# A Winograd-style convolution on one core: the last input pair through the SyncE queue, and paired stores

## The chip, the cores and the metric

The kernel runs on one NeuronCore of a Trainium2 chip. The core has TensorE (PE in the profile) for matmuls, VectorE (DVE), ScalarE (ACT), GpSimd (POOL) and SyncE (SP). Data moves between HBM and SBUF, the memory of 128 partitions on the core, through 16 DMA engines, which take their work from queues; here SyncE issues most transfers, and GpSimd can issue some, which may change the data type on the way. The metric is the device time of one execution in microseconds (us). Five runs before the change gave 127.62 to 128.03 us, with a median of 127.85.

## What is computed

A 3x3 convolution with padding 1 over 16 images of 64 channels and 64x64 pixels, to 128 channels, in fp32:

```python
def setup_inputs():
    batch, c_in, h, w, c_out = 16, 64, 64, 64, 128
    return {
        "x": np.random.randn(batch, c_in, h, w).astype(np.float32),
        "weight": np.random.randn(c_out, c_in, 3, 3).astype(np.float32) * 0.1,
    }

def reference(x, weight):
    x_pad = np.pad(x, ((0, 0), (0, 0), (1, 1), (1, 1)), mode='constant')
    ...
    output[b, co] += weight[co, ci, kh, kw] * x_pad[b, ci, kh:kh+h, kw:kw+w]
    ...
```

## The kernel before

The images are taken in 8 pairs. A pair fills the 128 partitions: 64 channels of the first image, then 64 of the second. A partition's row of one image is 64x64 fp32 values, 16 KB, so a pair of inputs is 2.1 MB; a pair of outputs is twice that, since there are 128 output channels, each in a partition of its own.

Two output rows are computed together from four input rows. The middle row of the kernel is applied once to the sum of two neighbouring rows (`ss`, made by `sums`, L93), and the result `ut` is added to two partial results, one for the even and one for the odd output row. The weights are combined to five sets `G0, G21, G1, G01, G2` in `Wt` (L103 to L124). Inputs of the matmuls are fp16, sums are fp32 in PSUM.

The loop at L135 runs over the pairs `p`, the loop at L146 over four blocks of 16 output rows. In a block, `group` (L149) issues the matmuls of L176 for both images: first `U` from `ss[p]`, then `A` and `Bt` from `xs[p]`, the pair in fp16. ScalarE copies `U` to `ut` (L190), VectorE adds `A + ut` (L196) and `Bt + ut` (L199) into the output tile `ots[p][b2]`, one tile for each image. Between these, ScalarE casts pieces of later pairs from fp32 to fp16 (`cast`, L66, in the order that `casts` lists at L129 to L133; two pieces go to GpSimd, L64), so that pair `p + 1` or `p + 2` is being cast while pair `p` is computed. GpSimd makes the sums of pair `p + 1` at the start of pair `p` (L140).

Transfers: SyncE loads the weights (L51), pair 0 in four cuts of rows, and pairs 1 to 6 in one transfer each (`load`, L55), all in fp32, ahead of everything else on its queue. Pair 7 comes another way: in pair 0, GpSimd issues one transfer that casts to fp16 on the way (`load_cast`, L78, called at L145) into the tile `xc`, so that no engine has to cast it, and GpSimd's sums for pair 7 read `xc`. When the fourth block of a pair is done, SyncE stores each image by a transfer of its own (L204); the last pair is stored in two halves of rows, so there are 14 stores of 2 MB and 4 of 1 MB. SyncE issues its transfers in the order written; a store waits for VectorE's last add.

Space: `big` has nine slots of 16 KB in each partition, handed out in turn by `next_slot` (L46). Pairs 0 to 6 take slots 0 to 6; the outputs take two slots a pair, beginning with 7 and 8 and then using again those of inputs that have been cast and of outputs that have been stored. `keep` holds the order of instructions on an engine as they are written.

Of the kernel before, what the change touches and what calls it, by code (L numbers as in the profile page):

```python
# [8 lines left out]
F32 = mybir.dt.float32  # L9
F16 = mybir.dt.float16  # L10
# [3 lines left out]
def kernel(  # L14
# [6 lines left out]
    nc = tc.nc  # L21
    B, CI, H, W = x.shape
    CO = weight.shape[0]
    assert H == 64 and W == 64 and CI == 64 and CO == 128 and B % 2 == 0
    NP = B // 2
    RB = 8

    keep = tc.keep_in_program_order
    x_rows = x.rearrange("b c h w -> (b c) h w")
    out_rows = out.rearrange("b co h w -> b co h w")  # L30
    w_flat = weight.rearrange("co ci kh kw -> co (ci kh kw)")

    const = ctx.enter_context(tc.tile_pool(name="const", bufs=1))
# [1 line left out]
    xpool = ctx.enter_context(tc.tile_pool(name="xpool", bufs=1))  # L35
    big = ctx.enter_context(tc.tile_pool(name="big", bufs=1))
# [2 lines left out]

    NH = 7
    slot = [0]

    def next_slot(shape, name):  # L46
        slot[0] += 1
        return big.tile(shape, F32, tag=f"slot{(slot[0] - 1) % 9}", name=name)

    w_raw = const.tile([CO, CI * 9], F32)  # L50
    nc.sync.dma_start(w_raw, w_flat)  # L51
    cuts = [(0, 18), (18, 34), (34, 50), (50, 64)]
    xf, xs = {}, {}

    def load(p):  # L55
        xf[p] = next_slot([128, H, W], "xf")
        for lo, hi in cuts if p == 0 else [(0, H)]:
            keep(
                nc.sync.dma_start(
                    xf[p][:, lo:hi, :], x_rows[128 * p : 128 * p + 128, lo:hi, :]  # L60
                )
            )
# [3 lines left out]
    def cast(p, n):  # L66
        if p not in xs:
            xs[p] = xpool.tile([128, H, W], F16, tag=f"xs{p % 4}", name="xs")
        lo, hi = cuts[n]
        copy = nc.gpsimd.tensor_copy if (p, n) in by_pool else nc.scalar.copy  # L70
        keep(copy(xs[p][:, lo:hi, :], xf[p][:, lo:hi, :]))  # L71

    ots = {}

    def outs(p):
        ots[p] = [next_slot([128, H // 2, 2, W], "ot") for _ in range(2)]

    def load_cast(p):  # L78
        xs[p] = xpool.tile([128, H, W], F16, tag="xc", name="xc")
        keep(nc.gpsimd.dma_start(xs[p], x_rows[128 * p : 128 * p + 128, :, :]))  # L80

    for p in range(NH):
        load(p)
    outs(0)
    ident = const.tile([128, 128], F16)
    make_identity(nc, ident)
# [6 lines left out]
    def sums(eng, p, src, lo, n):  # L93
        if p not in ss:
            ss[p] = spool.tile([128, H // 2, W], F16, tag="ss", name="ss")
        v = src.rearrange("p (j i) c -> p j i c", i=2)
        keep(
            eng.tensor_add(  # L98
                ss[p][:, lo : lo + n, :], v[:, lo : lo + n, 0, :], v[:, lo : lo + n, 1, :]
            )  # L100
        )
# [27 lines left out]
    casts = {p: [[]] * 4 for p in range(NP)}  # L129
    casts[0] = [[(0, 1)], [(0, 2), (0, 3)], [(1, 0), (1, 1)], [(1, 2), (1, 3)]]  # L130
    casts[1] = [[(2, 0), (2, 1)], [(2, 2), (2, 3)], [(3, 0), (3, 1)], [(3, 2)]]
    casts[2] = [[(4, 0), (4, 1)], [(4, 2), (4, 3)], [(5, 0), (5, 1)], [(5, 2)]]
    casts[3] = [[(6, n)] for n in range(4)]  # L133

    for p in range(NP):  # L135
        if p not in ots:
            outs(p)
        if p + 1 < NP:
            for lo in (0, 16):
                sums(nc.gpsimd, p + 1, xf[p + 1] if p < 2 else xs[p + 1], lo, 16)  # L140
            if p == 1 or p == 2:
                cast(2 * p + 1, 3)
        if p == 0:
            for q in range(NH, NP):
                load_cast(q)  # L145
        for blk in range(4):  # L146
            j0 = blk * RB

            def group(wi_rows):  # L149

                tiles = [
                    psum.tile([128, RB, W], F32, tag="acc", name="acc") for _ in range(2)
                ]
                n = 3 * len(wi_rows)
                i = 0
                for wi, off in wi_rows:
                    for kw in (1, 0, 2):
                        c_lo, c_hi = max(0, 1 - kw), min(W, W + 1 - kw)
                        for b2 in range(2):
                            p0 = 64 * b2  # L160
                            lo, hi = j0, j0 + RB
                            if off is None:
                                rhs = ss[p][p0 : p0 + 64, lo:hi, c_lo + kw - 1 : c_hi + kw - 1]
                            else:
                                while 2 * lo + off < 0:
                                    lo += 1
                                while 2 * (hi - 1) + off > H - 1:
                                    hi -= 1
                                first = 2 * lo + off
                                last = 2 * (hi - 1) + off  # L170
                                rhs = xs[p][
                                    p0 : p0 + 64,
                                    first : last + 1 : 2,
                                    c_lo + kw - 1 : c_hi + kw - 1,
                                ]
                            nc.tensor.matmul(  # L176
                                tiles[b2][:, lo - j0 : hi - j0, c_lo:c_hi],
                                Wt[p0 : p0 + 64, wi, kw, :],
                                rhs,
                                start=i == 0,  # L180
                                stop=i == n - 1,
                            )
                        i += 1
                return tiles

            U = group([(G1, None)])
            us = []
            for b2 in range(2):
                ut = upool.tile([128, RB, W], F32, tag="ut", name="ut")
                keep(nc.scalar.copy(ut, U[b2]))  # L190
                us.append(ut)
            for q, n in casts[p][blk]:
                cast(q, n)
            A = group([(G21, 1), (G0, -1)])
            for b2 in range(2):
                nc.vector.tensor_add(ots[p][b2][:, j0 : j0 + RB, 0, :], A[b2], us[b2])  # L196
            Bt = group([(G01, 0), (G2, 2)])
            for b2 in range(2):
                nc.vector.tensor_add(ots[p][b2][:, j0 : j0 + RB, 1, :], Bt[b2], us[b2])  # L199
            parts = {3: (0, 64)} if p < NP - 1 else {1: (0, 32), 3: (32, 64)}  # L200
            if blk in parts:
                lo, hi = parts[blk]
                for b2 in range(2):
                    keep(nc.sync.dma_start(  # L204
                        out_rows[2 * p + b2, :, lo:hi, :],
                        ots[p][b2].rearrange("p j i c -> p (j i) c")[:, lo:hi, :],
                    ))


# [1 line left out]
_INS = ['x', 'weight']  # L211
_OUTS = [((16, 128, 64, 64), 'float32')]
# [25 lines left out]
```

## Time and profile before

| | |
|---|---|
| median of five runs | 127.85 us |
| the profiled execution's own time | 127.98 us |
| its span, first to last instruction | 126.2 us |
| matmuls on TensorE, busy | 105.6 us (84%) |
| VectorE / ScalarE / GpSimd, busy | 84.4 / 61.8 / 33.6 us |
| DMA engines, mean over the span | 394 GB/s in 4,330 packets |
| HBM read / written | 17.07 / 33.55 MB |
| stores of one image (14) | 2,048 KB each, 20.8 us from issue to landing (median) |
| loads of one pair (6) | 2,048 KB each, 26.3 us from issue to landing (median) |
| cast of 128x1024 on ScalarE (mean of 26) | 1,066 ns |
| GpSimd's sums from fp32 / fp16 (128x1024) | 2,369 / 2,126 ns |
| GpSimd's issue of pair 7's transfer | 694 ns |

How to read it: the profile is one execution. The span is shorter than the execution's time by what lies around it. Busy shares are means over stages that differ, so one engine's share doesn't tell what sets the end. A transfer's time from issue to landing holds its wait behind earlier transfers. The page shows queues as q1 (SyncE's transfers), q0 (GpSimd's) and two more that fetch instructions. Besides the page, the trace keeps a record of every packet that a DMA engine moved, with its start, its length and its bytes; when a transfer is complete on one engine, that engine writes a packet of 4 bytes.

### The profile page before, as it was taken

The numbers are of one execution on the slowest core, as the hardware profiler recorded it, in microseconds if no ns is written. First come the engines' busy times: TensorE is split into PE (matmuls) and PEld (weight loads), VectorE is DVE, ScalarE is ACT, GpSimd is POOL, SyncE is SP. The second block draws the span as 40 slices with busy tenths as digits, with TensorE's granted clock in tenths as the row PEclk, the third lists the DMA queues.
The fourth block names the chain that finished last, engine by engine and source line by source line (L and its number), as shares of the span: only waits on it lengthen the run. The fifth ranks groups of instructions, "written<-read, shape, count | busy, mean of one in ns | idle before, by whom it ended". The sixth has DMA issues, their size and how long they took to land.

```text
span 126.2 us, 2439 instructions
## 1 busy us (share of the span) xinstructions
PE 105.6 (84%) x978; PEld 53.3 (42%) x978; DVE 84.4 (67%) x135; ACT 61.8 (49%) x94; POOL 33.6 (27%) x23
## 2 busy tenths in 40 slices
PE   0469999999999999999999999999999999930000
PEld 0324455545554455545554555445554545410000
DVE  0188777877777778777877787778777877770000
ACT  4174889998879886666333333333333333300000
POOL 2000298940762066006700570048000000000000
PEclk9999999999999999999999999999999999999555
DMA  4999999999999999999999999999999999999960
GB/s 122 278 442 441 431 426 431 353 322 325 377 426 434 416 444 416 431 426 426 431 436 426 431 416 431 442 426 421 426 431 442 426 421 416 434 410 431 426 262 13
DMA packets 4330, 49.72 MB, mean 394 GB/s; under 512 B 480, under 2 KB 480, under 8 KB 1120
## 3 DMA queue, kind: packets, MB, share of 16 engines
q1 hardware_dynamic: 4176, 48.53, 91.7%
q0 software_dynamic: 144, 1.05, 4.0%
q8 instruction: 7, 0.11, 0.3%
q14 instruction: 3, 0.02, 0.0%
HBM read 17.07 MB, written 33.55 MB: 401 GB/s over the span
## 4 chain that ended last, share of the span: by engine, by line
PE 82%; DMA 4%; DVE 2%; issue 1%; DVEq 0%; SPq 0%
PE acc L176 82%; DMA xf<-in_x_dram 4%; DVE ot L196 1%; DVE ss L98 1%; DVE ot L199 0%; DVEq L233 0%; SPq L51 0%; DVEq L196 0%
## 5 line engine op out<-in xcount | busy, mean ns | idle before, releaser
L176 PE MATMUL acc<-xs,Wt 64*128 64x504 f16 (+3 forms) x672 | 77.5, 377 | 0.0
L176 PEld LDWEIGHTS <-Wt 64*128 64x128 f16 x960 | 52.2, 95 | 53.6 <-issue 3.4
L196 DVE TENSOR_TENSOR ot<-acc,ut 128x512 f32<-128x512 f32 x64 | 41.2, 686 | 21.8 <-PE acc L176 18.2
L190 ACT COPY ut<-acc 128x512 f32<-128x512 f32 x64 | 34.4, 590 | 43.2 <-issue 39.0
L199 DVE TENSOR_TENSOR ot<-acc,ut 128x512 f32<-128x512 f32 x64 | 41.1, 685 | 0.0
L176 PE MATMUL acc<-ss,Wt 64*128 64x504 f16 (+1 forms) x192 | 27.0, 384 | 1.7 <-DVE ss L98 1.7
L71 ACT CAST xs<-xf 128x1024 f16<-128x1024 f32 (+2 forms) x26 | 26.7, 1066 | 1.2 <-DMA xf<-in_x_dram 1.2
L98 POOL TENSOR_TENSOR ss<-xs 128x1024 f16<-128x1024 f16 x8 | 16.8, 2126 | 26.2 <-PE acc L176 26.2
L98 POOL TENSOR_TENSOR ss<-xf 128x1024 f16<-128x1024 f32 x4 | 9.4, 2369 | 14.3 <-DMA xf<-in_x_dram 14.3
L176 PE MATMUL acc<-xc,Wt 64*128 64x504 f16 (+3 forms) x96 | 10.9, 373 | 0.0
L98 POOL TENSOR_TENSOR ss<-xc 128x1024 f16<-128x1024 f16 x2 | 4.2, 2130 | 8.6 <-issue 8.6
L116 PE MATMUL wp<-ident,w 128*64 128x128 f16 x18 | 1.3, 329 | 4.2 <-DVE w L88 4.2
L98 DVE TENSOR_TENSOR ss<-xf 128x512 f16<-128x512 f32 x4 | 2.8, 690 | 3.0 <-DMA xf<-in_x_dram 3.0
L71 POOL CAST xs<-xf 128x896 f16<-128x896 f32 x2 | 1.9, 930 | 4.5 <-DMA xf<-in_x_dram 4.5
L88 DVE CAST w<-w_raw 128x576 f16<-128x576 f32 x1 | 0.5, 461 | 3.7 <-DMA w_raw<-in_weight_dram 3.7
L116 PEld LDWEIGHTS <-w 128*64 128x64 f16 x18 | 1.1, 210 | 4.2 <-DVE w L88 4.2
L118 ACT CAST Wt<-wp 128x384 f16<-128x384 f32 x1 | 0.5, 479 | 2.9 <-PE wp L116 2.9
L118 ACT ACT_TABLE_LOAD x1 | 1.3, 1283 | 0.7 <-PEq L222 0.7
L123 ACT CAST Wt<-wp 128x384 f16<-128x384 f32 x1 | 0.5, 479 | 0.5 <-DVE Wt L121 0.5
L80 POOL DMA_DIRECT2D xc<-in_x_dram x1 | 0.7, 694 | 0.0
L120 DVE TENSOR_TENSOR Wt<-wp,Wt 128x384 f16<-128x384 f32 x1 | 0.5, 549 | 0.0
L121 DVE TENSOR_TENSOR Wt<-wp,Wt 128x384 f16<-128x384 f32 x1 | 0.5, 547 | 0.0
(7 smaller groups left out, 1.4 us busy)
## 6 DMA issues: line engine op xcount, KB each, us to landing
out_dram<-ot SPq DMA_DIRECT2D x14, 2048.0 KB, 20.8
xf<-in_x_dram SPq DMA_DIRECT2D x6, 2048.0 KB, 26.3
out_dram<-ot SPq DMA_DIRECT2D x4, 1024.0 KB, 12.0
xf<-in_x_dram SPq DMA_DIRECT2D x2, 512.0 KB, 6.5
xc<-in_x_dram POOLq DMA_DIRECT2D x1, 1024.0 KB, 15.2
xf<-in_x_dram SPq DMA_DIRECT2D x1, 576.0 KB, 5.3
xf<-in_x_dram SPq DMA_DIRECT2D x1, 448.0 KB, 7.5
w_raw<-in_weight_dram SPq DMA_DIRECT2D x1, 288.0 KB, 2.9
```

The lines of the kernel that those rows point to most:

```text
L71: keep(copy(xs[p][:, lo:hi, :], xf[p][:, lo:hi, :]))
L80: keep(nc.gpsimd.dma_start(xs[p], x_rows[128 * p : 128 * p + 128, :, :]))
L88: keep(nc.vector.tensor_copy(w16, w_raw))
L98: eng.tensor_add(ss[p][:, lo : lo + n, :], v[:, lo : lo + n, 0, :], v[:, lo : lo + n, 1, :])
L116: nc.tensor.matmul(wp[q : q + 64, k * CO : k * CO + CO], w16[:, t::9], ident)
L118: keep(nc.scalar.copy(wrow(G1), wps[1]))
L120: keep(nc.vector.tensor_sub(wrow(G21), wps[2], wrow(G1)))
L121: keep(nc.vector.tensor_sub(wrow(G01), wps[0], wrow(G1)))
L176: nc.tensor.matmul(tiles[b2][:, lo - j0 : hi - j0, c_lo:c_hi], Wt[p0 : p0 + 64, wi, kw, :], rhs, start=i == 0, stop=i == n - 1,)
L190: keep(nc.scalar.copy(ut, U[b2]))
L196: nc.vector.tensor_add(ots[p][b2][:, j0 : j0 + RB, 0, :], A[b2], us[b2])
L199: nc.vector.tensor_add(ots[p][b2][:, j0 : j0 + RB, 1, :], Bt[b2], us[b2])
```

## The change

Pair 7 is loaded by SyncE in fp32 like the others, into a tile of its own (`single`, 16 KB) that pair 6 has used before. Its load is issued right after pair 2's store, and ScalarE casts it in four pieces during pair 6; GpSimd's sums for pair 7 read the fp32 tile. GpSimd issues no transfer any more.

The nine slots become four of 32 KB and the single one. Pairs 0 and 1, 2 and 3, 4 and 5 share a slot each; an output pair has one slot for both images, in the order 3, 0, 1, 2, 3, 0, 1, 2. Both images of a pair are stored by one transfer, which takes 32 KB from each partition and writes 16 KB to each of the two images. There are 7 stores of 4 MB and 2 of 2 MB, and 21 transfers in all where there were 30.

```diff
-    out_rows = out.rearrange("b co h w -> b co h w")
+    out_pairs = out.rearrange("(g b) co h w -> g co b h w", b=2)
...
-    NH = 7
-    slot = [0]
-
-    def next_slot(shape, name):
-        slot[0] += 1
-        return big.tile(shape, F32, tag=f"slot{(slot[0] - 1) % 9}", name=name)
+    LATE = NP - 1
+
+    def pair_slot(n, shape, name):
+        return big.tile(shape, F32, tag=f"slot{n}", name=name)
...
+    two = {}
+
     def load(p):
-        xf[p] = next_slot([128, H, W], "xf")
+        if p >= 6:
+            xf[p] = big.tile([128, H, W], F32, tag="single", name="xf")
+        else:
+            if p % 2 == 0:
+                two[p // 2] = pair_slot(p // 2, [128, 2, H, W], "xf")
+            xf[p] = two[p // 2][:, p % 2, :, :]
...
     def outs(p):
-        ots[p] = [next_slot([128, H // 2, 2, W], "ot") for _ in range(2)]
-
-    def load_cast(p):
-        xs[p] = xpool.tile([128, H, W], F16, tag="xc", name="xc")
-        keep(nc.gpsimd.dma_start(xs[p], x_rows[128 * p : 128 * p + 128, :, :]))
-
-    for p in range(NH):
+        ots[p] = pair_slot((p + 3) % 4, [128, 2, H // 2, 2, W], "ot")
+
+    for p in range(LATE):
         load(p)
...
+    casts[6] = [[(7, n)] for n in range(4)]
...
-                sums(nc.gpsimd, p + 1, xf[p + 1] if p < 2 else xs[p + 1], lo, 16)
+                sums(nc.gpsimd, p + 1, xf[p + 1] if p in (0, 1, 6) else xs[p + 1], lo, 16)
...
-        if p == 0:
-            for q in range(NH, NP):
-                load_cast(q)
...
-                for b2 in range(2):
-                    keep(nc.sync.dma_start(
-                        out_rows[2 * p + b2, :, lo:hi, :],
-                        ots[p][b2].rearrange("p j i c -> p (j i) c")[:, lo:hi, :],
-                    ))
+                keep(nc.sync.dma_start(
+                    out_pairs[p, :, :, lo:hi, :],
+                    ots[p].rearrange("p b j i c -> p b (j i) c")[:, :, lo:hi, :],
+                ))
+                if p == 2:
+                    load(LATE)
```

More of the change, by code (lines that the diff above doesn't have):

```diff
@@ L195 @@
             for b2 in range(2):
-                nc.vector.tensor_add(ots[p][b2][:, j0 : j0 + RB, 0, :], A[b2], us[b2])
+                nc.vector.tensor_add(ots[p][:, b2, j0 : j0 + RB, 0, :], A[b2], us[b2])
             Bt = group([(G01, 0), (G2, 2)])
             for b2 in range(2):
-                nc.vector.tensor_add(ots[p][b2][:, j0 : j0 + RB, 1, :], Bt[b2], us[b2])
+                nc.vector.tensor_add(ots[p][:, b2, j0 : j0 + RB, 1, :], Bt[b2], us[b2])
             parts = {3: (0, 64)} if p < NP - 1 else {1: (0, 32), 3: (32, 64)}
```

## The prediction

> **What bounds the kernel now.** I read three views in this order: the page's slices and queues, a table of stretches that I asked of the trace, and the order of time around a few places. First the page: the busy tenths in 40 slices of 3.16 us, and below them the DMA queues with their share of 16 engines' span.
>
> ```profile
> PE   0469999999999999999999999999999999930000
> DMA  4999999999999999999999999999999999999960
> ...
> q1 hardware_dynamic: 4176, 48.53, 91.7%
> q0 software_dynamic: 144, 1.05, 4.0%
> ```
>
> TensorE is at 9 up to slice 36 and then has nothing to do; the DMA row stays at 9 from the second slice to the last but two, some 10 us longer. The chain of waits gives 82% to the matmuls of L176, and this misleads: it follows instructions back from the last one, and the end is not set there. The stretches show it (DMA share is the mean busy share of 16 engines, the matmul count stands in brackets).
>
> ```profile
> 90.00:105.00 15.00, 15.00 (x144) 7.54 (x141) 11.51 (x19) 5.20 (x10) 0.00 (x0) 1.00 1.00 427
> 105.00:112.00 7.00, 6.56 (x62) 3.11 (x58) 5.55 (x10) 2.15 (x4) 0.00 (x0) 1.00 1.00 425
> 112.00:119.00 7.00, 0.00 (x0) 0.00 (x0) 0.93 (x2) 0.00 (x0) 0.00 (x0) 0.82 1.00 421
> 119.00:121.00 2.00, 0.00 (x0) 0.00 (x0) 0.00 (x0) 0.00 (x0) 0.00 (x0) 0.50 0.99 418
> 121.00:122.00 1.00, 0.00 (x0) 0.00 (x0) 0.00 (x0) 0.00 (x0) 0.00 (x0) 0.50 0.58 246
> 122.00:123.00 1.00, 0.00 (x0) 0.00 (x0) 0.00 (x0) 0.00 (x0) 0.00 (x0) 0.50 0.29 123
> 123.00:124.00 1.00, 0.00 (x0) 0.00 (x0) 0.00 (x0) 0.00 (x0) 0.00 (x0) 0.50 0.06 25
> 124.00:125.00 1.00, 0.00 (x0) 0.00 (x0) 0.00 (x0) 0.00 (x0) 0.00 (x0) 0.50 0.04 16
> ```
>
> The 16 DMA engines are full until 121 us; TensorE, VectorE and ScalarE have finished by 113. Then the engines end one after another, and a share of 0.06 is one engine of 16: a single **late engine** sets the end. The trace's packet records (start, length, bytes) say why. A 16 KB packet takes 611 ns and the next begins 4 ns before its end, so 607 ns each. The punctual engines end at 120.9 us, engines that also fetched 16 KB of instructions (7 such packets, 878 to 1005 ns) later, two fetches giving 123.1, and the last at 124.66. That last engine runs its 16 KB store packets at 634 to 662 ns, from 45 us until the engines finish at 111.7; about 110 packets by 34 ns are 3.7 us, which is its whole lag. Its loads, and the 8 KB packets after 112, take the ordinary 611 and 309 ns.
>
> So the time is 1.8 us before the first packet (its start is at 1.75), the late engine's row of packets until 124.66, 1.5 us until the span ends, and 1.8 us around the span (127.98 for this execution). The median of the runs is 127.85, so I take 0.13 off what the sum gives. What can differ from no change by this measurement is 0.2%, 0.26 us.
>
> **The change, part by part.**
>
> *Pair 7 by SyncE in fp32.* It read 2.1 MB either way. By the page, q0 spent 4.0% of 126.2 = 5.05 us; q1 moves 48.53 MB in 115.7 us, so 2.1 MB cost it 5.00 us. By packets, the 128 of the cast, 8 on each engine, lasted 624 ns instead of 611: 8 x 13 = 0.10 us saved on every engine. About as many SyncE packets that took turns with them were 624 long too; overlaps take back most of that, so 0.05 to 0.20 us for the part, of which I take 0.12.
>
> *21 transfers in place of 30.* Each transfer ends on each engine with a 4-byte packet of 9.5 ns, and adds 6 ns to the row where it overlaps. Nine fewer: 0.05 to 0.09 us, taken as 0.08.
>
> One row of the skill speaks against storing two images by one transfer, because successive pieces of an engine then lie 2 MiB apart in HBM. The Trainium skill, page DMA: Bandwidth & Descriptors, section Latency and other measured facts, gives 164 GB/s for tiles whose rows lie 2 MiB apart; by that the 33.55 MB of stores would need 205 us, and the kernel some 250, an estimate from that page. In this case's trace the stores run at 421 to 431 GB/s with the 16 KB rows of 128 partitions lying one behind the other in HBM. The change keeps that between partitions, so I go by this row; no run here shows the paired pattern.
>
> *The load's place.* SyncE now issues it behind pair 2's store, and its slot is pair 6's, so it waits for ScalarE's last cast of pair 6. These lines are from the trace in order of time (start, duration):
>
> ```profile
> 58.85 0.95 ACT L71 CAST xs<-xf 128x896 f16<-128x896 f32 x1
> ...
> 83.59 4.21 POOL L98 TENSOR_TENSOR ss<-xc 128x1024 f16<-128x1024 f16 x2 [8.56 <-issue]
> ...
> 111.65 1.28 DVE L199 TENSOR_TENSOR ot<-acc,ut 128x512 f32<-128x512 f32 x2
> 112.36 1.50 SPq L204 DMA_DIRECT2D out_dram<-ot  x2
> ```
>
> The cast ends at 59.80; behind the waiting load on SyncE stand the stores of pairs 3 to 7, of which pair 3's is ready at 61.8, so none is held up. The DMA engines need work meanwhile. Before, a punctual engine ended the loads at 42.8, and each pair's stores at 52.6, 62.4, 72.1, 81.8, 91.5, 101.3, 111.0 (completion packets). Without the cast ahead of them, stores 0 to 2 move 4.9 us forward, to 47.7, 57.5 and 67.2; load 7, issued at 60, is there 7 us ahead of need and fills the gap until 72.1; store 3 follows as before. The stream has the same bytes and no hole. The load lands some 9 us before GpSimd's sums at 83.59. If the cover were gone, each us the cast came late would be a us of idle DMA.
>
> *One store where there were two.* It waits for the second image too. Pair 6's store was issued at 99.55 for the first image; the second image's add (the pair of L199 from 98.84, 1.28 us) ends at 100.1. The weight load was issued at 0.74 and its first packet ran at 1.75, so 1.0 us passes: a punctual engine that runs out at 101.05 gets work at 101.15, or 101.5 if issuing twice as many packets costs a second 332 ns. It may idle 0.1 to 0.45 us. The late engine is then still in store 5 until 104.7, so this costs the end nothing: cover 3.2 us. Pair 7's halves are ready earlier than any engine needs them (113.0 against 115.9).
>
> *Slots.* A pair's first add now waits for the whole store of four pairs earlier. The tightest is pair 7: store 3 lands by 84, the add is at about 100. Nothing.
>
> *ScalarE and GpSimd.* Four casts come into pair 6 (1.07 us mean, 4.3 in all), one to a block. Pair 3 has just this now: between 45 and 60 us TensorE is busy 15.00 of 15.00 us, so nothing stalls. GpSimd adds from fp32 (2.37 instead of 2.13 us, twice: 0.5 us) and no longer issues the transfer (0.7 us). Should pair 7 slip all the same, the cover at the end is the data still queued at 113: 8.9 us of mean engine work by the stretches, of which the last transfer's own is 16 x 0.306 = 4.9, so 4 us.
>
> The sum: 127.98 - 0.12 - 0.08 = 127.78, and less 0.13 is **127.65**; with the upper ends of both parts 127.56. I say 127.6.
>
> **The rivals.**
>
> *A, the late engine is no longer late* (faster). Its slow packets are stores alone, which the change re-forms, and nothing in the trace names the cause. Against it: they run from 45 to 111.7 us, long after the cast transfer landed at 34.5, and stop when the compute engines stop, which the change leaves as it is. The end would fall to the next engine, 123.12 in place of 124.66: 127.6 - 1.5 = 126.1. The Trainium skill, page DMA: Bandwidth & Descriptors, same section, says that DMA engines 7 and 15 are usually slower, and guesses at the descriptor rings of transfers issued by GpSimd; by it the removal would give about these 1.5 us, an estimate, and the time at which the slowness starts here disagrees.
>
> *B, dearer packets in paired stores* (slower). The engine alternates between two images. The late engine has 112 packets of 16 KB and 32 of 8 KB to store, worth 128 of 16 KB; each 6 ns (1%) more costs 0.78 us, and it decides from 2 ns on, where it eats the 0.2 saved. The row for another pattern is the 624 ns seen while two queues took turns: 128 x 13 = 1.7, so 129.3. For it speaks only that the pattern is new; against it, that 2,323 of 2,560 packets take exactly 611 ns, whether loads or stores.
>
> *C, an instruction fetch falls on the late engine* (slower). It cost 926 ns itself and made the packet behind it 1018 instead of 611: 1.3 us, so 128.9. Now none of the seven is among its packets; ScalarE's stream grows by eight instructions and others shrink, and TensorE's, the long one, stays, so little speaks for it.
>
> *D, the load blocks SyncE*: only if pair 6's cast slips 7 us. Left at nothing by the covers above.
>
> **How the numbers follow.** The forecast has 0.60, A 0.15, B with D 0.16, C 0.09. The forecast's own range is 127.4 to 127.9; it lies across the bound of 0.2% (127.59), so of its 0.60 some 0.27 count as faster, 0.31 as the same, 0.02 as slower. A is faster; B, C and D give 0.23 slower and 0.02 the same. Sums: faster 0.42, same 0.33, slower 0.25. The range reaches to A below, 126.0, and above to 128.5, the lower part of B and C, leaving some 0.18 out.
>
> **What would show it.** Right: q0 gone; 16 KB packets still at 611 ns; the DMA row full to 121 us; one engine alone in the last 1.5 us, its store packets at 634 to 662 ns; load 7 issued near 60 and landing near 72 to 75. Wrong: a 0 to 8 among the DMA tenths between the first and the last two slices; store packets of 615 ns or more on many engines; the last two engines ending within half a us.

## The result, and the profile after

The changed kernel takes 127.66 us (median of 53 runs, 127.35 to 128.56), the kernel before, in 95 runs beside it, 127.94 us. The ratio is 0.998, with a 95% interval of 0.9973 to 0.9988: 0.26 us faster, clear of noise and about the size of the bound of 0.2%. The profiled execution took 127.55 us, its span 125.8 us.

On the page of the changed kernel, the busy tenths in 40 slices and the queues:

```profile
PE   0489999999999999999999999999999999960000
DMA  4999999999999999999999999999999999999970
...
q1 hardware_dynamic: 4176, 50.63, 95.7%
q8 instruction: 7, 0.11, 0.3%
```

The queue q0 is gone and its bytes are on q1. The DMA row is full from the second slice to the last but two, as before. The stretches at the end (columns: stretch and length, PE, PEld, DVE, ACT and POOL busy with their counts, TensorE's granted clock, DMA share, GB/s):

```profile
90.00:105.00 15.00, 15.00 (x144) 7.63 (x142) 11.51 (x19) 8.10 (x13) 0.00 (x0) 1.00 1.01 428
...
119.00:121.00 2.00, 0.00 (x0) 0.00 (x0) 0.00 (x0) 0.00 (x0) 0.00 (x0) 0.50 1.03 438
121.00:122.00 1.00, 0.00 (x0) 0.00 (x0) 0.00 (x0) 0.00 (x0) 0.00 (x0) 0.50 0.64 270
122.00:123.00 1.00, 0.00 (x0) 0.00 (x0) 0.00 (x0) 0.00 (x0) 0.00 (x0) 0.50 0.18 74
123.00:124.00 1.00, 0.00 (x0) 0.00 (x0) 0.00 (x0) 0.00 (x0) 0.00 (x0) 0.50 0.08 33
124.00:125.00 1.00, 0.00 (x0) 0.00 (x0) 0.00 (x0) 0.00 (x0) 0.00 (x0) 0.50 0.00 0
```

ScalarE has 8.10 us of work between 90 and 105 instead of 5.20, the new casts (949 to 1,166 ns by their shape; the 1,066 ns given for 128x1024 is a mean over three shapes), and TensorE is still busy all 15 us. The end has the old shape: the engines run out from 121 us on, and in the last stretch with work a share of 0.08 is left, little more than one engine. The packet records give the last engine's end: 124.30 us in place of 124.66, with the next one at 122.85. Of 2,688 SyncE packets of 16 KB, 2,524 take exactly 611 ns; 112 from 42 us on take 628 to 672 ns, and the last of them starts at 111.4 us. The records don't name the engine, but 100 of the 112 follow each other without overlap and so fit on one engine; the other 12 overlap one of these.

The moved load, in order of time (start, duration, engine, line):

```profile
59.40 0.95 ACT L75 CAST xs<-xf 128x896 f16<-128x896 f32 x1
...
60.38 0.35 SPq L63 DMA_DIRECT2D xf<-in_x_dram  x1
...
84.15 4.68 POOL L98 TENSOR_TENSOR ss<-xf 128x1024 f16<-128x1024 f32 x2 [8.56 <-PE acc L174]
...
100.70 0.37 SPq L201 DMA_DIRECT2D out_dram<-ot  x1
```

SyncE issues the load as soon as pair 6's last cast has ended. GpSimd's sums for pair 7 wait for TensorE to free their buffer, as the bracket says, not for the load. By the semaphore records, which follow the 4-byte packets by 0.3 to 0.5 us, the first and last engines end store 0 at 48.0 and 50.2 us, store 1 at 57.7 and 59.8, store 2 at 67.4 and 69.5, the load at 72.3 and 74.5, and store 3 at 82.1 and 84.3. Each store of 4 MB now costs one issue of 0.37 us.

### The profile page after: what moved, and what is told of

Its sections match the earlier page's. It is cut to its first block, busy times and chain, and to the rows that moved or that the text cites. A ratio compares the mean times of both kernels' runs of the same rounds, so it can differ in the third digit from the quotient of the medians.

```text
span 125.8 us, 2424 instructions
## 1 busy us (share of the span) xinstructions
PE 106.6 (85%) x978; PEld 54.0 (43%) x978; DVE 84.3 (67%) x135; ACT 65.5 (52%) x98; POOL 33.4 (27%) x22
## 4 chain that ended last, share of the span: by engine, by line
PE 83%; DMA 4%; DVE 2%; issue 1%; DVEq 0%; SPq 0%
PE acc L174 83%; DMA xf<-in_x_dram 4%; DVE ot L194 1%; DVE ss L98 1%; DVE ot L197 0%; DVEq L230 0%; SPq L48 0%; DVEq L194 0%
## 5 line engine op out<-in xcount | busy, mean ns | idle before, releaser
L174 PE MATMUL acc<-xs,Wt 64*128 64x504 f16 (+3 forms) x768 | 89.4, 380 | 0.0
L174 PEld LDWEIGHTS <-Wt 64*128 64x128 f16 x960 | 52.9, 96 | 53.2 <-issue 3.9
L75 ACT CAST xs<-xf 128x1024 f16<-128x1024 f32 (+2 forms) x30 | 31.0, 1065 | 0.5 <-DMA xf<-in_x_dram 0.5
L98 POOL TENSOR_TENSOR ss<-xf 128x1024 f16<-128x1024 f32 x6 | 14.1, 2368 | 22.6 <-DMA xf<-in_x_dram 13.4
L118 ACT CAST Wt<-wp 128x384 f16<-128x384 f32 x1 | 0.5, 479 | 3.1 <-PE wp L116 3.1
L123 ACT CAST Wt<-wp 128x384 f16<-128x384 f32 x1 | 0.5, 479 | 0.5 <-DVE Wt L121 0.5
L124 ACT CAST Wt<-wp 128x384 f16<-128x384 f32 x1 | 0.5, 485 | 0.0
```

The costliest lines, as they stand in the source:

```text
L98: eng.tensor_add(ss[p][:, lo : lo + n, :], v[:, lo : lo + n, 0, :], v[:, lo : lo + n, 1, :])
L118: keep(nc.scalar.copy(wrow(G1), wps[1]))
L123: keep(nc.scalar.copy(wrow(G0), wps[0]))
L174: nc.tensor.matmul(tiles[b2][:, lo - j0 : hi - j0, c_lo:c_hi], Wt[p0 : p0 + 64, wi, kw, :], rhs, start=i == 0, stop=i == n - 1,)
```

## The experiments

Ratios are to the kernel before on the same chip in the same job, with 95% intervals. They differ a little from the quotient of the two medians, and the times in the table come from several chips. "Slow packets" are 16 KB packets of 628 to 672 ns that begin after 42 us; in a run with compute, 4 to 21 of them overlap others and so don't lie on the same engine. The ends are of the last engine and the one before it, in the profiled execution.

| run | time, us | ratio to before | slow packets | last two ends, us |
|---|---|---|---|---|
| before | 127.94 | 1 | 103 | 123.12, 124.66 |
| changed kernel | 127.66 | 0.998 (0.9973 to 0.9988) | 112 | 122.85, 124.30 |
| E1 load alone | 127.90 | 0.9995 (0.9977 to 1.0012) | 102 | 122.96, 124.79 |
| E2 pairs alone | 127.83 | 0.9983 (0.9967 to 0.9999) | 110 | 122.57, 124.73 |
| E3 load behind pair 4 | 131.20 | 1.0271 (1.0232 to 1.0309) | 110 | 127.28, 127.86 |
| E4 last store on 15 engines | 130.57 | 1.0193 (1.0159 to 1.0227) | 104 | 126.11, 126.73 |
| E5 transfers only | 126.18 | 0.9838 (0.9802 to 0.9875) | 3 | 122.49, 123.22 |
| E6 four casting transfers | 127.74 | 0.9976 (0.9964 to 0.9988) | 77 | 123.38, 124.03 |
| E7 load behind pair 3 | 127.74 | 0.9982 (0.9966 to 0.9998) | 99 | 122.78, 124.38 |
| E8 stores split again | 127.69 | 0.9987 (0.9967 to 1.0006) | 101 | 122.90, 124.44 |
| E9 second queue GpSimd | 128.18 | 1.0019 (1.0004 to 1.0034) | 93 | 123.14, 124.73 |
| E10 second queue ScalarE | 128.20 | 1.0015 (0.9997 to 1.0032) | 93 | 123.43, 124.95 |
| E11 four casts and pairs | 127.61 | 0.9968 (0.9951 to 0.9984) | 86 | 123.33, 124.11 |
| E12 changed kernel again | 127.61 | 0.9978 (0.9958 to 0.9998) | 101 | 122.93, 124.36 |

**E1 and E2: one part at a time.** E1 is the kernel before with pair 7 loaded by SyncE behind pair 2's stores, E2 has the paired stores and 32 KB slots, and pair 7 still by GpSimd.

```diff
 E1, on the kernel before
-        if p == 0:
-            for q in range(NH, NP):
-                load_cast(q)
...
+                if p == 2:
+                    load(NH)
 E2, on the changed kernel
+        if p == 0:
+            load_cast(LATE)
...
-                if p == 2:
-                    load(LATE)
```

> Pair 7 comes in fp32 through SyncE behind pair 2's stores, the stores stay one for each image (30 transfers). Theory (the row of packets on one late engine sets the end, and the cast transfer's 8 packets of 624 ns on it become 611 ns): 0.05 to 0.20 us faster than before, 127.75 to 127.9; the late engine ends 0.05 to 0.2 us earlier after its first packet than the 122.9 us of before. Rival (the gain comes from fewer transfers): no gain, 127.94.

> Paired stores from 32 KB slots, but pair 7 still by GpSimd's transfer with the cast (21 transfers). Theory: 0.05 to 0.09 us faster than before for nine completion packets fewer on each engine, so 127.85 to 127.9; punctual engines may idle up to 0.5 us near 101 us, the late engine doesn't. Rival (paired stores make packets dearer or cheaper): 16 KB store packets away from 611 ns, and 0.78 us of time for each 6 ns.

Both fall in the expected direction, by 0.06 and 0.22 us, and both intervals are wider than the effects. The last engine ends 0.13 us (E1) and 0.07 us (E2) later than in the kernel before, where E1 expected 0.05 to 0.2 us earlier; one profile each is too little for an effect of this size. E2's rival, dearer packets, falls: 2,298 of its 2,560 packets by SyncE are at 611 ns, and of the others most stand beside the cast (624) or on the late engine. How the 0.26 us divide can't be read from these two.

**E8: the pairing undone in the changed kernel.**

```diff
-                keep(nc.sync.dma_start(
-                    out_pairs[p, :, :, lo:hi, :],
...
+                for b2 in range(2):
+                    keep(nc.sync.dma_start(
+                        out_pairs[p, :, b2, lo:hi, :],
...
```

> The changed kernel with its stores undone to one for each image, from the same 32 KB slots (30 transfers). Theory: 0.05 to 0.09 us slower than the changed kernel, 0.9984 to 0.999 of before. Rival (the pairing brings the whole gain of 0.26 us): 1.000 of before, as E1 nearly gave.

E8 and E1 run the same stream of packets from differing slots. Their mean, 0.9991, leaves about 0.11 us for the load and 0.14 us for the pairing (0.9991 - 0.998 = 0.0011 of 128); the intervals of both reach from no effect to the whole. Neither rival is excluded. By the medians of the same jobs the division would be another: 0.9987 for E1 (127.90 to 128.07) and 0.9970 for E8 (127.69 to 128.08).

The mean of the 16 engines' last 4-byte packets says a little more. It is 122.15 us before, 122.07 in E1, 122.05 in E8, 121.92 in E2, and 122.04 and 121.99 in two profiles of the changed kernel. All are earlier, by 0.08 to 0.23 us, with one profile each; how the gain divides stays open.

**E7 and E3: the load one and two pairs later.**

```diff
-                if p == 2:
+                if p == 3:    # E7; E3 has 4
                     load(LATE)
```

> The changed kernel with pair 7's load behind pair 3's store, between the place of the change and that of E3 (behind pair 4's, 131.2). Theory (the place costs nothing as long as the load lands before its first use at 84 to 88 us): it lands at 81.8 on a punctual engine and at 84 to 85 on the late one; the time stays at 127.5 to 127.9. Rival (each step later costs, as a load among the stores delays them): 129 to 130.

> The changed kernel with pair 7's load behind pair 4's store. Theory (the place of the load is hidden, as the same packets run in another order): same time as the changed kernel, 127.66 within 0.15, and 0.2% below before. Rival (the late place is what gains, or a load among the stores costs): a difference of 0.3 us or more from the changed kernel in either direction.

E7 agrees; GpSimd's sums for pair 7 already wait there for the load, until 84.55 us. E3 doesn't, and my expectation there had left out that the load must land before its first use. Behind pair 4's store the load lands between 92.4 and 95.4 us, after its first use. E3's lines in order of time, and its stretches:

```profile
95.48 1.15 ACT L75 CAST xs<-xf 128x1152 f16<-128x1152 f32 x1 [7.14 <-DMA xf<-in_x_dram]
...
95.56 4.68 POOL L98 TENSOR_TENSOR ss<-xf 128x1024 f16<-128x1024 f32 x2 [19.93 <-DMA xf<-in_x_dram]
```

```profile
92.00:96.00 4.00, 1.60 (x16) 0.67 (x13) 0.00 (x0) 0.52 (x1) 0.44 (x1) 1.00 0.99 418
96.00:100.00 4.00, 2.72 (x13) 1.10 (x14) 2.48 (x4) 4.00 (x7) 4.00 (x2) 0.70 1.00 430
100.00:102.00 2.00, 2.00 (x16) 0.90 (x14) 1.40 (x3) 0.47 (x1) 0.23 (x1) 0.74 0.94 401
102.00:105.00 3.00, 3.00 (x32) 1.52 (x29) 2.27 (x4) 1.91 (x3) 0.00 (x0) 1.00 0.23 93
105.00:107.00 2.00, 2.00 (x24) 1.05 (x20) 1.40 (x4) 1.07 (x2) 0.00 (x0) 1.00 0.00 0
107.00:109.00 2.00, 2.00 (x22) 1.01 (x20) 2.00 (x4) 0.09 (x1) 0.00 (x0) 1.00 0.93 393
```

ScalarE stands 7.14 us before the cast, with the copies of `ut` queued behind it. So VectorE has nothing to add from 92 to 96, TensorE is down to 1.60 of 4 us, and pair 6's store is late. Only now do the DMA engines run out: share 0.23, then 0.00, near 102 to 107 us. The late engine has work until 104.98 and starts again at 107.34, and these 2.4 us are the larger part of the result. Another 0.7 us came before, where the load meets the stores: 20 packets between 89 and 93 us take 681 to 1,435 ns, two of them on the late engine. The last 0.5 us lie in store 6, whose packets stay slow on the late engine until 116.77, as TensorE works to 118.03. Up to pair 3's store no cost of the place shows; behind pair 4's it is 3.5 us.

This run also shows what slows the late engine. From 95.07 to 101.75 us its store packets take 611 ns, ten in a row, and one 615; from 101.75 on 634 to 661 again. In that stretch TensorE stands until 97.17 and then needs 4.89 us for 24 matmuls that otherwise take 2.69, while ScalarE and GpSimd are busy for all of 96 to 100 and VectorE for 2.48 us of it. So in this run the late engine is slow when TensorE works at its full pace, and the other three don't suffice.

**E4: leave one engine out of the last store.**

```diff
-                keep(nc.sync.dma_start(
-                    out_pairs[p, :, :, lo:hi, :],
...
+                for c0, c1 in [(0, 128)] if hi < H or p < NP - 1 else [(0, 120), (120, 128)]:
+                    keep(nc.sync.dma_start(
+                        out_pairs[p, c0:c1, :, lo:hi, :],
...
```

> The changed kernel, but the last store (32 rows of both images) goes as partitions 0 to 119, which makes 8 for each of 15 engines, and then 120 to 127. Theory (one late engine sets the end in every run, and it is the one that the 15 leave out): its last 16 packets of 306 ns fall away, so the next engines set the end: 0.8 to 1.4 us faster than the changed kernel, 126.3 to 126.9. Rival 1 (the late engine is among the 15): it gets up to 2 packets more, 0 to 0.6 us slower, 127.7 to 128.3. Rival 2 (the late engine is there only while the profile is taken): the profile ends 0.8 to 1.4 us earlier, the timed runs stay at 127.6 to 127.8.

```profile
117.00:119.00 2.00, 0.00 (x0) 0.00 (x0) 0.00 (x0) 0.00 (x0) 0.00 (x0) 0.50 1.00 315
119.00:121.00 2.00, 0.00 (x0) 0.00 (x0) 0.00 (x0) 0.00 (x0) 0.00 (x0) 0.50 0.90 266
...
122.00:123.00 1.00, 0.00 (x0) 0.00 (x0) 0.00 (x0) 0.00 (x0) 0.00 (x0) 0.50 0.77 205
```

Dearer by far than rival 1 allowed. The engines are busy at 0.90 to 1.00 and move only 266 to 315 GB/s: of the 305 packets of 8 KB that begin after 116 us, 102 take over 400 ns, 61 of them 590 to 640, about twice 309. Why is not shown. One engine has no work from 116.5 us, so it was a punctual one, not the late one. With the packets this dear, the run can't tell whether the late engine is there in runs without a profile.

**E5: the transfers without the computing.** All matmuls, casts and sums are left out.

```diff
-    ident = const.tile([128, 128], F16)
...
+    still = const.tile([128, 2, H, W], F32, name="still")
+    nc.vector.memset(still, 1.0)
+    for p in range(NP):
+        for lo, hi in [(0, 64)] if p < NP - 1 else [(0, 32), (32, 64)]:
+            keep(nc.sync.dma_start(out_pairs[p, :, :, lo:hi, :], still[:, :, lo:hi, :]))
+        if p == 2:
+            load(LATE)
```

> Only the transfers of the changed kernel, in its order, with the stores taken from one tile that VectorE fills once; no matmuls, casts or sums, so the output is constant. It asks where the late engine comes from. If from the compute engines' running (its slow packets stop at 111.4 us with them): no 16 KB store packet between 630 and 670 ns, the 16 engines end within 1 us, near 121 us, and the time is 124 to 125 us. If from the engine itself and its stores: the same 112 slow packets of about 646 ns, one engine 3 us behind, 127.3 to 127.8 us.

```profile
105.00:112.00 7.00, 0.00 (x0) 0.00 (x0) 1.00 0.99 425
...
121.00:122.00 1.00, 0.00 (x0) 0.00 (x0) 1.00 0.35 147
122.00:123.00 1.00, 0.00 (x0) 0.00 (x0) 1.00 0.08 33
123.00:124.00 1.00, 0.00 (x0) 0.00 (x0) 1.00 0.00 0
```

Three slow packets are left where there were over 100, so the slowness needs the computing. E5 alone doesn't prove it, as its stores also come from one tile and wait for no result. But where the computing ends in the other kernels, 16 KB packets go on: in the kernel before, the late engine's last nine of them take 662, 652, 644 and 644 ns up to TensorE's end at 111.56 us, then 619, 620, 621, 615 and 611. E3's pause agrees. The time fell only to 126.18 us, not to 124 to 125. At 121 to 122 us a share of 0.35 is still left: the engines still end over 2.5 us, 120.75 to 123.22. Near 71 us, between the load and the stores, the records show a burst of 14 packets of 700 to 1,359 ns, which kept some engines back. The time lies in neither expected range. So the transfers alone set all but 1.5 us of the changed kernel's time.

**E6: four casting transfers.** Pairs 4 to 7 by GpSimd; the casts of pairs 4 to 6 by ScalarE and GpSimd are left out.

```diff
-    NH = 7
+    NH = 4
...
-    by_pool = [(3, 3), (5, 3)]
+    by_pool = [(3, 3)]
...
-    casts[2] = [[(4, 0), (4, 1)], [(4, 2), (4, 3)], [(5, 0), (5, 1)], [(5, 2)]]
-    casts[3] = [[(6, n)] for n in range(4)]
```

> The kernel before with pairs 4 to 7 (in place of 7 alone) through GpSimd's casting transfer, and the casts of ScalarE and GpSimd for them left out. Theory (each such transfer costs each engine 0.05 to 0.20 us more than a plain one, and the DMA row sets the end): three more give 0.15 to 0.60 us slower than before, 128.1 to 128.7. Rival (a casting transfer costs the same as a plain one, as E1's 0.9995 allows): within 0.1 us of before.

Neither: it is 0.31 us faster than before. E6's page and its end:

```profile
GB/s 128 310 407 453 427 427 422 300 284 336 321 300 341 341 292 321 336 300 315 393 427 438 427 417 427 433 443 422 433 417 427 433 427 438 425 409 422 427 341 26
...
q0 software_dynamic: 576, 4.19, 16.2%
```

```profile
121.00:122.00 1.00, 0.00 (x0) 0.00 (x0) 0.00 (x0) 0.00 (x0) 0.00 (x0) 0.50 0.70 295
122.00:123.00 1.00, 0.00 (x0) 0.00 (x0) 0.00 (x0) 0.00 (x0) 0.00 (x0) 0.50 0.41 172
123.00:124.00 1.00, 0.00 (x0) 0.00 (x0) 0.00 (x0) 0.00 (x0) 0.00 (x0) 0.50 0.10 41
```

The casts last from 23 to 63 us, so from the first store on they run beside stores, where the single cast of before ran beside loads. The price is there: 634 ns for a cast's packet in the mean, 624 for most packets beside it, and more engines at work between 121 and 123 us (0.70 and 0.41 against 0.58 and 0.29 before). But from 36 to 58 us not one store packet is between 630 and 700 ns, so there are 77 slow packets in place of 103, and the last end comes at 124.03. ScalarE's lighter work is not the reason: it is busy 32% of the time from 36 to 58 us and 34% from 63 to 100, when the slow packets are back.

This run also bears on which engine sets the timed end. The mean of the 16 last packets is 122.36 us, 0.22 us later than before, as the casts' price would have it, and the runs are 0.31 us faster: they follow the last engine, not the mean one.

**E9 and E10: plain transfers on two queues.** If taking turns spares the late engine, two queues of plain stores should.

```diff
-                keep(nc.sync.dma_start(
...
+                for b2, queue in ((0, nc.sync), (1, nc.gpsimd)):
+                    keep(queue.dma_start(
+                        out_pairs[p, :, b2, lo:hi, :],
...
```

> The changed kernel with the first image of each pair stored by SyncE and the second by GpSimd (plain fp32, no cast), so that packets of two queues alternate on every engine. New theory (E6: while two queues alternate, no 16 KB store packet was over 624 ns for lack of a late one, and a pair of starts was 612 ns apart): the late engine is no longer late, every engine pays 5 ns more for each of 128 packets, 0.65 us; the last engines are those that fetched instructions, near 123.5 us in place of 124.3: 126.5 to 127.2 us. Rival (the late engine stays late in its stores whatever the queue): 0.3 to 0.7 us slower than the changed kernel, 128.0 to 128.4.

> As E9, but the second image's store is issued by ScalarE, in the next pair behind its first copies of U. New theory: as E9 if it takes only two queues, 126.5 to 127.2 us. Rival (what spares the late engine is GpSimd's way of issuing): slow packets of 640 to 650 ns stay, 127.5 to 128.0 us. ScalarE's wait in its stream is met before it is reached and costs nothing; if not, VectorE's adds shift and a hole shows in the DMA row.

E9's end, and its second queue:

```profile
q0 software_dynamic: 1296, 16.78, 31.3%
...
122.00:123.00 1.00, 0.00 (x0) 0.00 (x0) 0.00 (x0) 0.00 (x0) 0.00 (x0) 0.50 0.34 139
123.00:124.00 1.00, 0.00 (x0) 0.00 (x0) 0.00 (x0) 0.00 (x0) 0.00 (x0) 0.50 0.06 25
124.00:125.00 1.00, 0.00 (x0) 0.00 (x0) 0.00 (x0) 0.00 (x0) 0.00 (x0) 0.50 0.04 16
```

The idea falls, and with it the reading of 624 ns as the price of taking turns. Plain packets keep their 611 ns (2,517 of 2,688) on two queues, 93 slow ones stay, and the last engine is alone again from 123 us on. E9's rival is what came; E10 keeps its slow packets too and lies 0.2 us above its rival's range. What spared the late engine in E6 belongs to the casting loads; whether it is the cast, or that they are loads where E9 and E10 add stores, is open. The runs are 0.2% slower than before (E10's interval holds no effect) and 0.35 to 0.4% slower than the changed kernel.

**E11 and E12: the two gains together.** E6 with the paired stores, and the changed kernel beside it.

> E6's four casting transfers (pairs 4 to 7) together with the paired stores of the change. If what E6 gained (0.9976: the late engine spared about 26 slow packets while casts and stores alternate) and what the pairing gains (0.998 against 0.9991 of E1 and E8 together, 0.14 us) add up: 0.9965 of before, 127.5 to 127.7 us, ahead of both kernels. If they don't add: 0.9975 to 0.998, the same as the changed kernel.

> The changed kernel itself, on the chip of the run beside it, so that the two can be compared directly: 0.998 of before, 0.9965 to 0.9995 in this many rounds; one engine behind the others by 1.3 to 1.7 us at the end.

Both medians are 127.61 us, and 0.9968 and 0.9978 have overlapping intervals. E11 is faster than the kernel before; that it is faster than the changed kernel isn't shown. E12 is where it was expected, with its last engine 1.43 us behind the next. E11's mean end is 122.40 us against E12's 121.99, at the same time of the runs: again the time goes with the last engine (124.11 and 124.36) rather than with the mean one.

## Why the prediction was right, point by point

**What bounds it** held. The transfers alone take 126.18 us (E5), and compute that slipped lengthened the kernel for the most part by the time that the DMA engines ran dry (E3). That the last engine sets the end, and not the mean one, the timed runs of E6 and E11 bear out.

**The stream without a hole** held within 0.2 us: stores 0 to 2 were put at 47.7, 57.5 and 67.2 us and the load at 72.1 on a punctual engine, by the 4-byte packets; those of the first engine end at 47.6, 57.3, 67.1 and 72.0. It left out that packets can grow dear where the load meets the stores: four of 705 to 1,152 ns from 69.8 to 72.1 us in the changed kernel. Punctual engines do idle near pair 6's store: issued at 100.70, it leaves a mean of 14.7 engines at work for half a us at 101. This was put at 0.1 to 0.45 us, on engines that don't set the end, and the late engine wasn't among them.

**The sum**, 0.20 us with 0.25 taken from its upper part, met 0.26. That they agree to 0.01 us is luck, as the interval reaches from 0.15 to 0.35 us. Its two terms are not confirmed one by one. The cast's 0.12 was priced by packets of 624 ns instead of 611; that length is real, but E6 shows that casts beside stores also spare the late engine, so more casts gave a shorter time. For the single cast beside loads, E1 and E8 leave 0.11 us with no effect inside their intervals. The 0.08 of nine fewer completions stands beside about 0.14 from the pairing, as unsure.

**Rival A**, the late engine cured, fell: without any transfer by GpSimd it has some 100 slow packets, and the last end is 1.45 us behind the next. The Trainium skill's guess (page DMA: Bandwidth & Descriptors, section Latency and other measured facts), descriptor rings of GpSimd's transfers, doesn't fit here; which of the 16 is late, the records don't say. TensorE's running is needed for it (E5, E3's pause); by which way is open.

**Rival B** fell: 2,524 packets at 611 ns. The 164 GB/s in the same section of the skill are for successive partitions 2 MiB apart in HBM. The paired store has this step only between the two pieces of one partition, and costs nothing that shows: the DMA engines move 428 GB/s between 90 and 105 us.

**Rival C** was not seen: seven fetches of 16 KB of 882 to 981 ns between 19 and 101 us, and the late engine's lag is as before.

**Rival D** was left at nothing for the load's place behind pair 2, rightly, and E3 shows its price when the load is two pairs later.

## What to carry to other kernels

Where the DMA row is full to the end, a moved transfer is free as long as two dates hold: it is issued before the queue behind it runs dry, and it lands before its first use, counted with all that stands ahead of it on the queue (no cost seen at 84 us here, 3.5 us at 95). Look at the last stretches engine by engine: a share of 0.06 for a microsecond or two is one engine. Work taken from the other fifteen should then gain nothing; E6 and E11 fit, where the mean engine works 0.2 and 0.4 us longer and the time is no longer. Parts of 0.1 us can't be told apart by twelve runs whose interval is 0.3% wide; their sum could, by fifty.

## What the runs showed of the hardware that was not expected

One DMA engine moves most of its 16 KB store packets in about 646 ns instead of 611 while TensorE works, in every kernel here with compute. It is back at 611 while TensorE pauses and then runs slowly (E3, 95 to 101 us, with the other engines busy), and within five packets behind TensorE's end (619 down to 611 ns in the kernel before); with no compute at all it isn't slow (E5). Nor is it while casting loads run beside the stores (E6), though TensorE is busy throughout; beside plain stores on either second queue it is (E9, E10).

Packets can take twice their time and more where a load meets stores on one queue (705 to 1,152 ns in the changed kernel, 681 to 1,435 in E3, against 611).

After a store of 120 partitions in place of 128, with one engine out of work, a third of the 8 KB packets took over 400 ns, many 596 or 633, against 309 (E4).
